# Half-row matmuls in turns on both row halves, and an RWKV chunk inverse applied ahead of the recurrence

## The chip, the cores and the metric

The kernel runs on one core of a Trainium2 chip. The metric is device time in microseconds (us) of one execution. Durations below come from one profiled execution of the kernel before, unless a sentence says that they are medians of several runs.

## What is computed

Two layers of a hybrid decoder trunk on 512 tokens of width 1024, all in float32. Each layer is a token mixer of four head groups, cross-attention into 256 memory tokens, and a SwiGLU FFN; a last RMS norm follows.

```
for each layer:
    p = rms_norm(x) @ w_in
    y = concat(rglru(p_a), retention(p_b), rwkv7(p_c), ssd(p_d))
    x = x + y @ w_out
    x = x + cross_attention(rms_norm(x), mem)
    x = x + (silu(h @ w_gate) * (h @ w_up)) @ w_down,  h = rms_norm(x)
out = rms_norm(x) * norm_final
```

The change is mostly in the RWKV-7 group, four heads of width 64. Per token and head its state S obeys

```
sa = S @ (-kk);   S = S * w + sa (kk*a)^T + v k^T;   y = S @ r
```

Retention rotates q and k: the two 32-row halves of each head are exchanged, multiplied by a sine table and added to the product with the cosine table.

## The kernel before

**Dense products.** Every large product is three fp32r matmuls (high and low parts, `mm3`, L677): a weight tile of 1024 x 128 is loaded by SyncE (SP) into a `u` buffer, ScalarE casts its high part to `v`, VectorE subtracts the low part into `w` (`weights`, L662), and 24 matmuls of 512 columns accumulate into an `a` bank of PSUM (`project`, L687). There are three buffers of each kind. The dense matmuls of the program form one chain in program order.

**Everything else on TensorE** is small plain float32 work in `b` banks (five of them): transposes, sums and the products of the mixers. A float32 matmul is two MATMUL instructions in the trace. Products with 64 rows of contraction use one half of the array's rows (form 64*128 or 64*64 in the profile), those with 64 outputs one half of its columns (128*64 or 64*64).

**Order.** Calls only record operations. `Sched.order` (L433) is a list planner with a cost for each operation; it picks the next operation of every engine by its modelled start, class and longest path to the end, gives out the buffers, and writes a fixed order for each engine. So one engine's instructions never overtake each other, and all instructions carry the source line of the helper that issues them, L569; groups are told apart by tile names and shapes. A `b` bank is only given out when two others stay free, unless the operation is the next in program order (`place`, L541).

**RWKV.** `rwkv_pair` (L1131) runs for two pairs of heads. Two low-rank products (`zw`, `za`, L1137) take lower and upper row halves; eight 64-row products per half of the tokens build the matrices inside the 64-token chunks (L1192 to L1201), first all of one head, then all of the other, each head with a bank of its own. `rwkv_solve` (L1232) inverts 32 x 32 triangles on GpSimd and carries the result (`rf`) and its transpose (`rt`) through DRAM to two tiles each. `rwkv_whole` (L1289) completes the 64 x 64 inverses by two products per cell (16 cells for each pair). `rwkv_scan` (L1310) walks over the eight chunks; for each chunk:

```
1348   E.matmul(zb[:, ...], pairs[i][0][hf][:, ccol], st[i], ...)              # state into z and y
1350   E.matmul(zb[rw[i], oc(i, o)], pairs[i][1][hf, o][:, zcol], u[:, i, hd(o)], ...)
1351   V.tensor_copy(z[rw[0]], zb[rw[0], 0:P])
1355   E.matmul(ub[rw[i], oc(i, o)], Rs[i][rw[i], n * HD:...], z[rw[i], hd(o)], ...)
1356   A.copy(u[rw[0], 0], ub[rw[0], 0:P])
1361   E.matmul(ub[:, sc], pairs[i][2][hf][:, ccol], u[:, i], ...)              # new state
1364   V.scalar_tensor_tensor(new, ub[:, sc], w, self.con("bones"), ...)
1369   E.matmul(zb[ry[i], oc(i, o)], pairs[i][1][hf, o][:, ycol], u[:, i, hd(o)], ...)
```

**Retention** (L1041) exchanges the 32-row blocks with four SP DMAs for each of four tiles (L1057), and in each of four chunks forms the scores of two heads on the lower rows and then of two on the upper rows (L1074 to L1078).

**Last norm** (`finish`, L1602). The token halves are finished one after the other. For each, sums over partitions (L1625, L1626), a root on ScalarE, a transpose that spreads it to all partitions (L1638), a ScalarE copy of it to `rb` (L1640), eight multiplies of 128 x 256 shared by VectorE (tiles 0, 2, 4, 6, 7) and GpSimd (1, 3, 5), and four SP DMAs to the output (L1648).

Of the kernel before, what the change touches and what calls it, by code (L numbers as in the profile page):

```python
# [14 lines left out]
ALU = mybir.AluOpType  # L15
# [219 lines left out]
class Op:  # L235
    __slots__ = ("n", "eng", "fn", "args", "kw", "dur", "lat", "preds", "succ", "left", "ready", "end", "rank", "cls",
                 "roots", "first", "chain", "bytes", "start", "table", "grid", "port", "fine")
# [27 lines left out]
KINDS = {"s": (T, 71), "n": (1024, 1), "t": (16, 64), "q": (P, 14), "u": (KD * P + 16, 3), "v": (KD * P + 16, 3), "w": (KD * P + 16, 3),  # L265
# [3 lines left out]
class Sched:  # L269
# [94 lines left out]
    @staticmethod  # L364
    def area(x):
        return (0, 1, 0, 1) if x.root.kind == "d" else x.box()
# [11 lines left out]
    def cost(self, op, fn, out, ins):  # L378
# [3 lines left out]
        op.table = op.grid = None  # L382
# [8 lines left out]
        elif op.eng == "PE":  # L391
# [4 lines left out]
            else:  # L396
# [7 lines left out]
                if min(k, m) <= HD:  # L404

                    op.dur /= 2
        elif op.eng == "ACT":
# [25 lines left out]
    def order(self, reserve):  # L433
# [27 lines left out]
        grid = P, P  # L461
# [4 lines left out]
        while len(out) < len(ops):  # L466
            best = None
            for e, lst in avail.items():
                c = clock[e]
                pick, pt = None, INF  # L470
                for op in lst:
# [9 lines left out]
                    key = (t, op.cls if op.cls != 2 or side < 1500.0 else 0, op.grid != grid if e == "PE" else False, -op.rank, op.n)  # L481
# [19 lines left out]
            if e == "PE" and op.grid != grid:  # L501
                t += self.change(grid, op.grid)
                grid = op.grid
            end = clock[e] = t + op.dur
# [67 lines left out]
class Trunk:  # L572
    def __init__(self, ctx, tc, a):
# [9 lines left out]
        self.d = {}  # L583

# [456 lines left out]
    def retention(self, l, proj, vals):  # L1041
# [8 lines left out]
        for which in range(2):  # L1050
            for i in range(2):
# [13 lines left out]
        for j in range(4):  # L1065
# [65 lines left out]
    def rwkv_pair(self, l, i, lora, wa, k, r, v, nd):  # L1131
# [5 lines left out]
        for z, rw in ((zw, slice(0, HD)), (za, slice(HD, P))):  # L1137
            self.mm3(z, [x[rw, cs] for x in lora], [x[rw] for x in wa], True, True)
# [53 lines left out]
        for hf in range(2):  # L1192
            for o in range(2):
                b = self.bank()
                rw = slice(HD * o, HD * o + HD)
                for c in range(4):
                    cc = slice(c * P, (c + 1) * P)
                    E.matmul(b[:, cc], bk[hf][rw, cc], ar[hf][rw, cc], start=True, stop=True)
# [33 lines left out]
    def rwkv_solve(self, l, nd):  # L1232
# [41 lines left out]
        return res  # L1274
# [471 lines left out]
```

## Time and profile before

| what | us |
|---|---|
| median of three runs | 1658.06 (1657.96 to 1658.47) |
| the profiled execution | 1656.97 |
| its span, first to last instruction | 1655.2 |
| TensorE busy | 1626.0 |
| VectorE busy | 1015.0 |
| ScalarE busy | 640.0 |
| GpSimd busy | 67.1 |

The profiled execution is 1.77 us longer than its span and 1.09 us shorter than the median. The granted TensorE clock over the span was 0.995 of full speed. Matmuls are pipelined and overlap in the trace, so what one costs is the step from its start to the next start.

### The profile page before, as it was taken

The numbers are of one execution on the slowest core, as the hardware profiler recorded it, in microseconds if no ns is written. First come the engines' busy times: TensorE is split into PE (matmuls) and PEld (weight loads), VectorE is DVE, ScalarE is ACT, GpSimd is POOL, SyncE is SP. The second block draws the span as 40 slices with busy tenths as digits, with TensorE's granted clock in tenths as the row PEclk, the third lists the DMA queues.
The fourth block names the chain that finished last, engine by engine and source line by source line (L and its number), as shares of the span: only waits on it lengthen the run. The fifth ranks groups of instructions, "written<-read, shape, count | busy, mean of one in ns | idle before, by whom it ended". The sixth has DMA issues, their size and how long they took to land.

```text
span 1655.2 us, 21468 instructions
## 1 busy us (share of the span) xinstructions
PE 1626.0 (98%) x8344; PEld 1329.1 (80%) x8344; DVE 1015.0 (61%) x1816; ACT 640.0 (39%) x988; POOL 67.1 (4%) x140
## 2 busy tenths in 40 slices
PE   7999999999999999999999999999999999999997
PEld 6787778888788888888888877888888888888886
DVE  8867699666565454533478678977565654544333
ACT  7434355444343232322354344554444322322221
POOL 0024000000000000000000600000000000000001
PEclk9999999999999999999999999999999999999999
DMA  9345203523233333233463442144233333333331
GB/s 283 114 102 123 76 26 88 180 77 87 82 99 89 101 90 102 86 106 115 133 179 99 110 99 58 52 140 141 64 90 91 100 89 102 89 97 88 92 101 56
DMA packets 315078, 169.57 MB, mean 102 GB/s; under 512 B 40160, under 2 KB 302560, under 8 KB 314848
## 3 DMA queue, kind: packets, MB, share of 16 engines
q1 hardware_dynamic: 314976, 168.19, 35.5%
q8 instruction: 66, 1.08, 0.3%
q14 instruction: 36, 0.29, 0.1%
HBM read 156.63 MB, written 9.44 MB: 100 GB/s over the span
## 4 chain that ended last, share of the span: by engine, by line
PE 92%; DVE 2%; DMA 2%; ACT 1%; SPq 1%; issue 0%; DVEq 0%; ACTq 0%
PE a L569 84%; PE b L569 9%; DVE s L569 2%; SPq L569 1%; ACT s L569 1%; DMA u<-in_mem_wk_dram 1%; DMA u<-in_w_in_dram 1%; DVE w L569 0%; DMA s<-fd 0%; DVE t L569 0%; ACT v L569 0%; DMA s<-in_memT_dram 0%; DMA s<-s 0%; ACT n L569 0%; DVEq L1742 0%
## 5 line engine op out<-in xcount | busy, mean ns | idle before, releaser
L569 PE MATMUL a<-s,v 128*128 128x512 f32 (+1 forms) x4012 | 1237.2, 388 | 8.5 <-ACT s L569 6.3
L569 PEld LDWEIGHTS a<-s,v 128*128 128x128 f32 x4012 | 741.5, 189 | 166.6 <-ACT s L569 6.9
L569 PE MATMUL a<-s,w 128*128 128x512 f32 (+1 forms) x2006 | 776.6, 387 | 0.6 <-DVE w L569 0.6
L569 ACT CAST v<-u 128x1024 fp32r<-128x1024 f32 (+3 forms) x275 | 282.6, 1028 | 663.2 <-PE a L569 380.5
L569 PEld LDWEIGHTS a<-s,w 128*128 128x128 f32 x2006 | 378.4, 189 | 80.9 <-issue 1.8
L569 DVE TENSOR_TENSOR w<-u,v 128x1024 fp32r<-128x1024 f32 (+3 forms) x275 | 329.5, 1199 | 163.6 <-ACT v L569 162.6
L569 DVE TENSOR_TENSOR s<-a,s 128x512 f32<-128x512 f32 (+1 forms) x132 | 90.6, 690 | 263.3 <-PE a L569 242.2
L569 ACT ACTIVATE s<-s 128x512 f32<-128x512 f32 (+3 forms) x233 | 144.3, 628 | 121.0 <-DVE s L569 113.7
L569 DVE TENSOR_TENSOR s<-s,s 128x512 f32<-128x512 f32 (+4 forms) x223 | 140.8, 639 | 18.2 <-ACT s L569 13.5
L569 PE MATMUL b<-s,s 128*64 128x64 f32 (+8 forms) x1268 | 134.6, 270 | 6.2 <-DVE s L569 3.5
L569 PEld LDWEIGHTS b<-s,s 128*128 128x128 f32 (+3 forms) x1268 | 111.5, 167 | 34.4 <-issue 9.1
L569 DVE SCALAR_TENSOR_TENSOR s<-s,s 128x512 f32<-128x512 f32 (+2 forms) x168 | 111.4, 669 | 10.9 <-ACT s L569 10.1
L569 DVE TENSOR_TENSOR s<-s,a 128x512 f32<-128x512 f32 (+1 forms) x49 | 33.2, 677 | 92.5 <-PE a L569 92.5
L569 PE MATMUL a<-v,s 128*128 128x260 f32 (+1 forms) x256 | 67.5, 344 | 0.0
L569 DVE SCALAR_TENSOR_TENSOR s<-s,prm,s 128x512 fp32r<-128x512 f32 (+3 forms) x78 | 53.1, 697 | 3.5 <-ACT s L569 3.1
L569 ACT COPY s<-b 64x128 f32<-64x128 f32 (+3 forms) x92 | 29.9, 335 | 63.3 <-PE b L569 47.4
L569 DVE SCALAR_TENSOR_TENSOR s<-a,prm,s 128x511 f32<-128x511 f32 (+2 forms) x64 | 47.7, 745 | 2.3 <-ACT s L569 1.4
L569 PEld LDWEIGHTS a<-v,s 128*128 128x128 f32 x256 | 44.3, 188 | 5.7
L569 PE MATMUL b<-cst,s 128*128 128x128 f32 (+2 forms) x312 | 46.3, 263 | 2.2 <-DVE s L569 1.1
L569 PEld LDWEIGHTS b<-cst,s 128*128 128x128 f32 x312 | 38.9, 157 | 9.7 <-DVE s L569 2.4
L569 PE MATMUL a<-w,s 128*128 128x512 f32 (+1 forms) x128 | 43.7, 342 | 0.0
L569 ACT CAST s<-s 128x512 fp32r<-128x512 f32 x48 | 29.1, 621 | 34.0 <-DVE s L569 27.4
(92 smaller groups left out, 667.6 us busy)
## 6 DMA issues: line engine op xcount, KB each, us to landing
u<-in_ffn_w_in_dram SPq DMA_DIRECT2D x88, 512.0 KB, 3.7
u<-in_w_in_dram SPq DMA_DIRECT2D x52, 512.0 KB, 3.8
u<-in_ffn_w_out_dram SPq DMA_DIRECT2D x32, 512.0 KB, 3.9
u<-in_mem_wv_dram SPq DMA_DIRECT2D x16, 512.0 KB, 3.6
u<-in_w_out_dram SPq DMA_DIRECT2D x16, 512.0 KB, 4.0
u<-in_mem_wq_dram SPq DMA_DIRECT2D x16, 512.0 KB, 3.9
u<-in_mem_wo_dram SPq DMA_DIRECT2D x16, 512.0 KB, 3.9
u<-in_mem_wk_dram SPq DMA_DIRECT2D x13, 512.0 KB, 4.0
```

What stands on the lines that cost most here:

```text
L569: op.fn(*[real(x) for x in op.args], **{k: real(x) for k, x in op.kw.items()})
```

## The change

- Row halves in turns: in `rwkv_pair` the three low-rank products of `zw` and `za` alternate; the 64-row products of two heads alternate, with two banks taken together (`hold`); retention's scores likewise. The planner also prefers, among small matmuls of one form, one on another part of the array than the last.
- `rwkv_solve` carries `rf` through DRAM ahead of `rt`.
- `rwkv_whole` now forms the whole inverse (its other quarter copied into a unit matrix `unit`, ScalarE) and multiplies it into the rows of `at` and `bt` that the recurrence reads, for each pair 16 + 16 + 32 products of 64 x 64 in place of 16 + 16, with ScalarE copies in between.
- `rwkv_scan`: the z products of all chunks go ahead of the recurrence (`zv`); a chunk then has a state product, an addition on VectorE, the product to the new state and its scaling; the y products follow once for each four chunks and are added on VectorE.
- Rotary exchanges are issued by ScalarE.
- Last norm: all eight multiplies on VectorE, straight from PSUM; no ScalarE copy; output DMAs in turns from SP and ScalarE; the sums that don't need the last tile come first.

```diff
-KINDS = {... "q": (P, 14), ...
+KINDS = {... "q": (P, 6), ...
+    def hold(op, x):
+        op.roots.append(x.root)
+        op.first.append(x.root)
+        x.root.uses += 1
...
-                    key = (t, ..., op.grid != grid if e == "PE" else False, -op.rank, op.n)
+                    key = (t, ..., (op.grid != grid, op.part is not None and op.part == part) if e == "PE" else (), -op.rank, op.n)
...
-                    self.Q.dma_start(s[o:o + 32], c[32 * b:32 * b + 32])
+                    A.dma_start(s[o:o + 32], c[32 * b:32 * b + 32])
...
-            for o in range(2):
-                b = self.bank()
-                rows = slice(HD * o, HD * o + HD)
-                for i in range(2):
-                    E.matmul(b[:, i * P:(i + 1) * P], k[i][rows, tk], q[i][rows, tk], start=True, stop=True)
+            bs = self.bank(), self.bank()
+            for i in range(2):
+                for o, b in enumerate(bs):
+                    rows = slice(HD * o, HD * o + HD)
+                    op = E.matmul(b[:, i * P:(i + 1) * P], k[i][rows, tk], q[i][rows, tk], start=True, stop=True)
+                    if i == o == 0:
+                        self.s.hold(op, bs[1])
...
-        for z, rw in ((zw, slice(0, HD)), (za, slice(HD, P))):
-            self.mm3(z, [x[rw, cs] for x in lora], [x[rw] for x in wa], True, True)
+        for n, (a, b) in enumerate(((0, 0), (0, 1), (1, 0))):
+            for z, rw in ((zw, slice(0, HD)), (za, slice(HD, P))):
+                E.matmul(z, lora[a][rw, cs], wa[b][rw], start=(n == 0), stop=(n == 2))
...
-        for k, f in enumerate((rt, rf)):
+        for k, f in ((1, rf), (0, rt)):
...
-            V.tensor_tensor(x[:, c2::2]..., b..., self.con("lower")..., op=ALU.mult)
+        for c3 in range(2):
+            p0 = rows(c3).start + 32
+            A.copy(x[p0:p0 + 32]..., b[p0:p0 + 32]...)
         b = self.bank()
         for c in cells:
-            E.matmul(b[rows(c[3]), col(c)], x[rows(c[3]), col(c)], R[rows(c[3]), col(c)], start=True, stop=True)
-        V.tensor_tensor(R, b, R, op=ALU.add)
+            E.matmul(b[rows(c[3]), col(c)], R[rows(c[3]), col(c)], x[rows(c[3]), col(c)], start=True, stop=True)
+        inv = TT
+        A.copy(inv, b)
+        for hf in range(2):
+            b = self.bank()
+            for q in range(2):
+                for o in range(2):
+                    for rw, e in cells:
+                        E.matmul(b[rw, ...], inv[rw, col((hf, o, q))], bt[hf][rw, x0:x0 + HD], start=True, stop=True)
+                    for rw, e in cells:
+                        E.matmul(b[rw, ...], inv[rw, col((hf, o, q))], at[hf, o][rw, self.ycol(i, q, e)], start=True, stop=True)
+            for c3 in range(2):
+                A.copy(bt[hf][rw]..., b[rw, 0:2 * P]...)
+            for c3 in range(2):
+                for o in range(2):
+                    A.copy(at[hf, o][rw]..., b[rw, 2 * P + o * P:2 * P + (o + 1) * P]...)
...
+            for q in range(2):
+                for o in range(2):
+                    for e in range(2):
+                        for i in range(2):
+                            E.matmul(b[rw[i], ...], pairs[i][1][hf, o][ry[i], self.zcol(i, q, e)], uv[hf, e][ry[i], i, q, hd(o)], start=True, stop=True)
+            A.copy(zv[:, hf], b)
...
+                if c:
+                    E.matmul(b[:, ic], pairs[i][0][hf][:, ccol], st[i], start=True, stop=True)
+                    V.tensor_tensor(u[rw[i], i], b[rw[i], ic], zc, op=ALU.add)
+                    A.copy(yt[i][ry[i], q * P:(q + 1) * P], b[ry[i], ic])
...
+                    E.matmul(b[:, sc], pairs[i][2][hf][:, ccol], u[:, i], start=True, stop=True)
...
+            if c % 4 == 3:
+                b = self.bank()
+                ...
+                                E_ = E.matmul(b[ry[i], ...], pairs[i][1][hf, o][:, self.ycol(i, x, e)], uv[hf, e][:, i, x, hd(o)], start=True, stop=True)
+                for i in range(2):
+                    V.tensor_tensor(yt[i]..., yt[i]..., b..., op=ALU.add)
...
-            rb = self.S()[:, :H]
-            A.copy(rb, b[:, :H])
...
-                    if j + k in shared:
-                        G.tensor_tensor(t[:, k], xg[j + k][:, ts], rb, op=ALU.mult)
-                    else:
-                        V.scalar_tensor_tensor(t[:, k], ..., rb, op0=ALU.mult, op1=ALU.mult)
-                self.Q.dma_start(out[...], t)
+                    V.scalar_tensor_tensor(t[:, k], ..., b[:, :H], op0=ALU.mult, op1=ALU.mult)
+                (A if j % 4 else self.Q).dma_start(out[...], t)
```

## Rows read from the trace of the kernel before

**Rows 1.** The page: busy engines, and the chain that ended last.

```profile
PE 1626.0 (98%) x8344; PEld 1329.1 (80%) x8344; DVE 1015.0 (61%) x1816; ACT 640.0 (39%) x988; POOL 67.1 (4%) x140
...
PE 92%; DVE 2%; DMA 2%; ACT 1%; SPq 1%; issue 0%; DVEq 0%; ACTq 0%
```

**Rows 2.** TensorE's waits over the span: total us, times, longest.

```profile
PE a L569 <- ACT s L569: 6.3, 2, 5.7
PE b L569 <- DVE s L569: 4.6, 6, 1.9
...
PE b L569 <- DMA s<-fd: 1.9, 2, 1.7
```

**Rows 3.** Timeline of TensorE, layer 0, 64-row groups: start, us, instruction, count.

```profile
71.64 0.40 PE L569 MATMUL a<-s,v 128*128 128x512 f32 x1
71.96 1.83 PE L569 MATMUL b<-s,s 64*128 64x128 f32 x28
73.72 0.49 PE L569 MATMUL a<-s,v 128*128 128x512 f32 x1
...
97.03 1.71 PE L569 MATMUL b<-s,s 64*128 64x128 f32 x16
98.66 0.39 PE L569 MATMUL a<-v,s 128*128 128x260 f32 x1
...
251.71 0.71 PE L569 MATMUL b<-s,s 64*128 64x128 f32 x4
252.35 0.51 PE L569 MATMUL a<-s,v 128*128 128x512 f32 x1
252.69 0.39 PE L569 MATMUL a<-s,w 128*128 128x512 f32 x1
252.92 0.63 PE L569 MATMUL a<-s,v 128*128 128x512 f32 x2
```

**Rows 4.** The same timeline, 64-column products of the RWKV group, both layers.

```profile
161.93 0.24 PE L569 MATMUL b<-s,s 64*64 64x64 f32 x1 [1.69 <-DMA s<-fd]
...
181.02 0.45 PE L569 MATMUL b<-q,s 64*64 64x64 f32 x8
181.40 0.50 PE L569 MATMUL a<-s,v 128*128 128x512 f32 x1
...
975.12 1.73 PE L569 MATMUL b<-s,s 64*64 64x64 f32 x52
976.78 0.50 PE L569 MATMUL a<-s,v 128*128 128x512 f32 x1
```

**Rows 5.** Dense matmuls (a) alone in a recurrence step, and around the low-rank products.

```profile
181.02:186.50 5.48, 4.05 (x13) 2.03 (x12) 0.00 (x0) 0.00 (x0) 1.00 0.34 96
...
49.70:53.60 3.90, 1.27 (x4) 0.52 (x4) 0.00 (x0) 0.00 (x0) 1.00 0.17 50
```

**Rows 6.** Busy us by stretch: PE, PEld, DVE, ACT, POOL, then clock and DMA.

```profile
150.00:210.00 60.00, 57.47 (x481) 43.60 (x479) 39.83 (x93) 22.07 (x51) 0.00 (x0) 0.97 0.41 90
210.00:290.00 80.00, 79.38 (x479) 64.27 (x476) 77.78 (x216) 44.35 (x76) 0.00 (x0) 1.00 0.21 61
```

**Rows 7.** Timelines: last split of a mixer output, and w_out's first matmuls.

```profile
289.56 0.69 DVE L569 SCALAR_TENSOR_TENSOR s<-s,s 128x512 fp32r<-128x512 f32 x1
...
289.43 0.63 PE L569 MATMUL a<-s,v 128*128 128x512 f32 x2
```

**Rows 8.** Timelines of the tail, and instruction groups of VectorE for its multiplies.

```profile
1643.12 0.83 PE L569 MATMUL b<-cst,s 128*128 128x1 f32 x6 [0.96 <-ACT s L569]
...
1645.76 0.37 ACT L569 COPY s<-b 128x256 f32<-128x256 f32 x1 [1.37 <-PE b L569]
...
1649.75 1.98 SPq L569 DMA_DIRECT2D out_dram<-s  x4
...
L569 DVE SCALAR_TENSOR_TENSOR s<-s,prm,s 128x256 fp32r<-128x256 f32 x16 | 7.3, 481 | 1.1 <-ACT s L569 0.8
...
DMA to landing us min/median/max: 2.2/2.7/3.0
```

More of the change, by code (lines that the diff above doesn't have):

```diff
@@ L236 @@
     __slots__ = ("n", "eng", "fn", "args", "kw", "dur", "lat", "preds", "succ", "left", "ready", "end", "rank", "cls",
-                 "roots", "first", "chain", "bytes", "start", "table", "grid", "port", "fine")
+                 "roots", "first", "chain", "bytes", "start", "table", "grid", "part", "port", "fine")
 def _free(x):
@@ L381, in cost @@
         op.bytes = 0
-        op.table = op.grid = None
+        op.table = op.grid = op.part = None
         op.port = False
@@ L460, in order @@
         side = wire = 0.0
-        grid = P, P
+        grid, part = (P, P), None
         held = {"DVE": 0.0, "POOL": 0.0}
@@ L480, in order @@
                         t = self.place(op, t, reserve)
-                    key = (t, op.cls if op.cls != 2 or side < 1500.0 else 0, op.grid != grid if e == "PE" else False, -op.rank, op.n)
+                    key = (t, op.cls if op.cls != 2 or side < 1500.0 else 0, (op.grid != grid, op.part is not None and op.part == part) if e == "PE" else (), -op.rank, op.n)
                     if pick is None or key < pick:
@@ L500, in order @@
                 r.slot = fr.pop(i)[1]
[L501 to L504, printed above, removed]
+            dur = op.dur
+            if e == "PE":
+                if op.grid != grid:
+                    t += self.change(grid, op.grid)
+                grid, part = op.grid, op.part
+            end = clock[e] = t + dur
             if op.port:
@@ L583, in __init__ @@
         self.d = {}
+        self.unit = [None, None]
     def S(self, dt=F32):
@@ L1192, in rwkv_pair @@
         for hf in range(2):
[L1193 to L1198, printed above, removed]
+            bs = self.bank(), self.bank()
+            for c in range(4):
+                cc = slice(c * P, (c + 1) * P)
+                for o in range(2):
+                    rw = slice(HD * o, HD * o + HD)
+                    op = E.matmul(bs[o][:, cc], bk[hf][rw, cc], ar[hf][rw, cc], start=True, stop=True)
+                    if c == o == 0:
+                        self.s.hold(op, bs[1])
+            for o, b in enumerate(bs):
                 t = self.S()
@@ L1273, in rwkv_solve @@
         self.solved = done
-        return res
+        return [r[::-1] for r in res]
     @staticmethod
@@ L1298, in rwkv_whole @@
             E.matmul(b[rows(c[3]), col(c)], at[c[0], c[1]][rows(c[3]), self.zcol(i, c[2], c[3] ^ i)], TT[rows(c[3]), col(c)], start=True, stop=True)
-        x = self.S()
-        for c2 in range(2):
-            V.tensor_tensor(x[:, c2::2].rearrange("p (n k w) -> p n k w", n=8, k=2), b.rearrange("p (n k c w) -> p n k c w", n=8, k=2, c=2)[:, :, :, c2],
-                            self.con("lower")[:, c2::2].rearrange("p (k w) -> p k w", k=2).unsqueeze(1).to_broadcast([P, 8, 2, 16]), op=ALU.mult)
+        if l == 0:
+            self.unit[i] = self.s.fixed([P, T], f"unit{i}")
+            V.memset(self.unit[i], 0.0)
+            for c3 in range(2):
+                rw = rows(c3)
+                A.copy(self.unit[i][rw].rearrange("p (n x) -> p n x", n=8), self.con("ident")[rw, rw].unsqueeze(1).to_broadcast([HD, 8, HD]))
@@ L1602, in finish @@
     def finish(self, xs, out):
[L1604 removed]
+        V, A, E = self.V, self.A, self.E
         ones = self.con("ones")[:, 0:1]
[L1606 to L1609 removed]
         s = None
@@ L1624, in finish @@
             for j in range(2):
-                E.matmul(b[:, j:j + 1], s[:, n * H + j * P:n * H + (j + 1) * P], ones, start=True, stop=False)
-                E.matmul(b[:, j:j + 1], sq[:, j * P:(j + 1) * P], ones, start=False, stop=True)
+                E.matmul(b[:, j:j + 1], s[:, n * H + j * P:n * H + (j + 1) * P], ones, start=(j == 0), stop=False, skip_group_check=True)
+            for j in range(2):
+                E.matmul(b[:, j:j + 1], sq[:, j * P:(j + 1) * P], ones, start=False, stop=True, skip_group_check=True)
             v = self.tiny()[:, :2]
```

98 lines of the change are left out of this document (55 added, 43 removed).

## The prediction

> **What bounds the kernel now.** I read the page first. TensorE is busy for 1626 of 1655.2 us and carries 92% of the chain that ended last [rows 1], so a change moves the time by what it takes from TensorE's queue, by what TensorE waits, and by what follows its last dense matmul. The waits come second: the longest single one, 5.7 us, is the start; beyond it TensorE waited 4.6 us for VectorE and 1.9 us for the solved blocks coming back from DRAM [rows 2]. So almost everything to win is small float32 work that stands between dense matmuls, and its cost is read from timelines by steps from start to start.
>
> A dense matmul of 512 columns steps 0.232 us (252.69 to 252.92). Into a group with 64 rows the step is 0.32 (71.64 to 71.96), and the first dense step after one is 0.34 (252.35 to 252.69) [rows 3]. So each such group costs about 0.2 us outside itself. With that added, 8 products of 64 x 64 cost 0.58 and 52 cost 1.86, so 0.029 each and 0.35 for the change of form, 0.15 of it inside the group [rows 4]. Taking 0.15 off, 28 products of 64 rows took 1.61, 0.058 each; four of one head took 0.49, 0.12 each; 16 took 1.48, 0.093 each [rows 3]. Where the trace has two heads' products in turns on the two row halves they already run side by side, a pair in 0.115; where one head follows the other they take that time singly.
>
> One whole recurrence step is the stretch from 181.02 to 186.50. Of its 13 dense matmuls one began before it, so 12 x 0.232 = 2.78 us are dense and 5.48 - 2.78 = 2.70 us are side work [rows 5].
>
> **The change part by part.**
>
> *Low-rank products in turns.* The stretch of 3.90 us around them holds four dense matmuls, of which the last begins at its end; less three steps, 0.70, they cost 3.2 us [rows 5]. After: two groups of three pairs, 2 x (3 x 0.232 + 0.35) = 2.1. Gain 1.1 a layer, 2.2 us in all (bounds 0 and 2.6).
>
> *The 64-row products of `rwkv_pair`.* 64 MATMULs a layer; all in turns they cost 32 x 0.115 = 3.7 plus 0.35 for each of two to four groups, 4.4 to 5.1. Before, 28 of them already stood in turns at 1.96 with their change of form; at the rate of the group of 16 the other 36 cost 3.3 plus 0.35 for each of two groups or more, 6.0 together. I take 1.0 a layer, 2.0 us (0 to 3.6).
>
> *Retention's scores.* Eight groups of four a layer at 0.64 + 0.2 = 0.84 [rows 3], 6.7 us if each stands alone, become four groups of eight, 4 x 0.115 + 0.35 = 0.81 each, 3.2. Some of the eight will have shared a change of form, so I take 2.5 of the 3.5: 5.0 us for both layers (0 to 7).
>
> *Recurrence.* Before, eight steps of 2.70, less a state product in the first and a new state in the last (0.46 each: four MATMULs of full form, which the rows don't price singly, taken at the 0.115 of a 64-row one with as many columns): 20.7 us a layer. After, a step has four MATMULs for the state product and four for the new state, no change of form, 0.92, seven times: 6.4; the y products come as two groups of 32 at 0.029 plus 0.35, 2.6. That saves 11.7 a layer. It is paid ahead of the recurrence: z products, 64 in two groups, 2 x (0.93 + 0.35) = 2.6; and `rwkv_whole` goes from 128 MATMULs to 256, 128 x 0.029 = 3.7 more and one more change of form, 0.35. Net 11.7 - 6.7 = 5.0 a layer, 10.0 us. If the z products don't pair, because they cross from one row half to the other column half, 64 x 0.029 = 1.9 a layer is lost; if the y products share their form with others, up to 1 is won.
>
> Here one rule speaks against the change. In the trace 52 products of 64 x 64, which write two halves of the same bank in turns, cost 0.029 each [rows 4]. The Trainium skill, page "TensorEngine Tiling (Array Packing)", section Restrictions and Gotchas, says that different row tiles cannot access the same PSUM bank simultaneously. The trace does not agree with it where the outputs lie on different partitions, and I go by the trace; what serial products would give stands among the rivals.
>
> *Waits ahead of the recurrence.* `rf` going first brings the tile that the first product needs earlier; the wait for it was 1.69 us in layer 0 [rows 4], and all such waits are at most 4.6 + 1.9 us [rows 2]. Against that, two more rounds of product and ScalarE copy stand in the chain of each layer; at the same wait for each, 4 x 1.69 = 6.8 lost. Between -6.8 and +6.5 I take 3 us won, as the wait in the rows is the one that goes.
>
> *Tail.* Before, SP's first output DMA was issued at 1649.75, after VectorE's last multiply, and the fourth landed 3.0 us after an issue that ended the row at 1651.73 [rows 8]: the four wait in one queue for the last multiply. After, the multiplies start where the ScalarE copy started, 1645.76. Eight at 7.3/16 = 0.456 us (the same form with nobody on GpSimd) end at 1649.4; only the last pair's DMA is left, landing 2.2 us later, 1651.6, where the fourth landed at about 1651.3 + 3.0 = 1654.2 before. Two of six sum matmuls no longer stand behind the last square, 0.83/6 x 2 = 0.28 [rows 8]. Gain 2.8 us. A multiply that reads PSUM has no row in this shape: at 0.3 us slower each it would take the gain back to 0.4.
>
> *At no cost.* The rotary exchanges leave SP, whose queue cost TensorE little; on ScalarE 32 issues at 1.98/4 = 0.5 us [rows 8] are 16 us beside an engine busy 22 of 60 us in that stretch [rows 6]. What covers them is the weight casts being ahead by up to three buffers. The unit tiles and the smaller pool cost nothing on TensorE.
>
> The sum: 2.2 + 2.0 + 5.0 + 10.0 + 3 + 2.8 = 25.0 us. From the profiled execution, 1656.97, that gives 1632.0; from the median, which stands 1.09 higher, 1633.1, rounded **1633**.
>
> **The rivals.**
>
> *VectorE ends the mixer.* From 210 to 290 it is busy for 77.8 of 80 us, though only 39.8 of 60 before that [rows 6]. The last split of a mixer output starts at 289.56 and takes 0.69; `w_out` begins at 289.43, and reaches the last quarter of its 24 matmuls 18 x 0.232 = 4.2 later, at 293.6 [rows 7]. So the slack is 3.4 us, and a layer's 11.1 us of gain needs 8 of the 20 us that VectorE idles before 210. A recurrence that is over sooner gives its work back there, which speaks for the forecast. If nothing moves, the layers gain 2 x 3.4 and the tail 2.8: 1648.5.
>
> *TensorE waits at each stage.* The inverse is now four stages of product, ScalarE copy, product. Should the fixed order hold TensorE at each for as long as it waited at 161.93, 1.69 us [rows 4], that is 2 x 4 x 1.69 = 13.5, and the 3 us are lost too: 1649.6. For it: this wait exists now. Against: dense work stands ready, and the planner knows the copies.
>
> *The pairs don't come.* Taking two of five banks at once, with two kept free, may make the planner break them up. Then 2.2 + 2.0 + 5.0 is lost: 1642.3.
>
> *Products into one bank run singly.* The z products read one row half and write the other's partitions, for which there is no row. Were all 320 products of 64 x 64 a layer to take two turns where the 52 took one, 0.058 each [rows 4], 2 x 9.3 us more make 1651.7.
>
> *ScalarE's queue turns it slower.* Each burst of four exchanges stands in order ahead of weight casts; if it waits for its tile, casts come late and TensorE starves. There are eight bursts; to be slower by over 0.2% they must hold TensorE for 25.0 + 3.3 us, 3.5 each, after three buffers of lead have gone. At 5 us each the result is 1673. That ScalarE is idle two thirds of the time [rows 6] speaks against it.
>
> **How the numbers follow.** The forecast has 0.64, with a range of its own from 1625 to 1640 by the bounds above; VectorE 0.10, waits 0.12, no pairs 0.07, one bank 0.02, the slower case 0.05. Some 0.2% (3.3 us) is about what a measurement can tell from no change. The range 1621 to 1646 reaches below by a dozen changes of form that the planner may merge, at 0.35 each, and above to the milder forms of the rivals. Faster 0.93; within 0.2% 0.03, where two rivals add up; slower 0.04.
>
> **What would show it.** Right: matmuls of form 64*128 in groups of eight in retention at some 0.8 us; a recurrence step with under 1 us of side work; 64*64 products at about 0.03 us; output DMAs from two queues, the last issued near 4 us after the spreading transposes. Wrong: TensorE idle ahead of the first recurrence step or before `w_out`; casts of weights behind ScalarE's DMA issues; 64*64 products at 0.05 us. The prediction falls if TensorE's waits grow by over 10 us, or if the changes of form are not fewer.

## The result, and the profile after

The changed kernel takes **1643.18 us** (median of 4, 1642.39 to 1644.17) beside 1658.01 for the kernel before on the same chip: ratio 0.9911, 95% interval 0.9899 to 0.9923. It is 14.8 us faster where 25.0 were forecast. The profiled execution took 1642.86 us, with a span of 1641.1. Lines have moved by eleven: L569 is now L580. In the views below, rows between two shown ones may be left out.

The page, busy engines, chain and the DMA queue of ScalarE:

```profile
PE 1614.6 (98%) x8472; PEld 1321.8 (81%) x8472; DVE 1005.1 (61%) x1816; ACT 648.7 (40%) x1015; POOL 63.3 (4%) x134
q10 hardware_dynamic: 2624, 3.15, 0.7%
PE 92%; DVE 3%; ACT 2%; DMA 2%; ACTq 1%; issue 1%; SPq 0%; DVEq 0%
```

Beside [rows 1], TensorE executes 128 matmuls more and is busy for 11.4 us less. The kernel is still bound by TensorE's queue. The waits of TensorE over the whole span (total us, times, longest), as in [rows 2]:

```profile
PE a L580 <- ACT s L580: 5.8, 1, 5.8
...
PE b L580 <- DVE s L580: 4.8, 7, 1.2
...
PE b L580 <- ACT s L580: 1.9, 5, 1.0
...
PE b L580 <- DMA s<-fd: 1.3, 2, 1.1
```

The DRAM wait got shorter, from 1.9 to 1.3, and the small products' waits for VectorE did not (4.6 before, 4.8 now). The timelines of TensorE (start, us, instruction, count, idle before) show where they went, and the groups that answer to [rows 3] and [rows 4]:

```profile
73.72 1.83 PE L580 MATMUL b<-s,s 64*128 64x128 f32 x28
...
158.77 0.30 PE L580 MATMUL b<-unit,s 64*64 64x64 f32 x2 [0.27 <-DMA s<-fd]
...
164.70 1.73 PE L580 MATMUL b<-s,s 64*64 64x64 f32 x52
...
177.84 0.38 PE L580 MATMUL b<-q,s 128*128 128x128 f32 x2
177.98 0.48 PE L580 MATMUL a<-s,w 128*128 128x512 f32 x1
178.30 0.39 PE L580 MATMUL a<-s,v 128*128 128x512 f32 x1
...
189.69 1.15 PE L580 MATMUL b<-s,s 128*64 128x64 f32 x32
193.80 0.49 PE L580 MATMUL b<-q,s 128*128 128x128 f32 x2 [1.17 <-DVE s L580]
...
209.40 0.71 PE L580 MATMUL b<-s,s 64*128 64x128 f32 x8
...
857.18 0.73 PE L580 MATMUL b<-s,s 64*128 64x512 f32 x3
...
858.27 1.19 PE L580 MATMUL b<-s,s 64*128 64x512 f32 x6
...
860.27 0.95 PE L580 MATMUL b<-s,s 64*128 64x512 f32 x3
```

Retention's eight products now take 0.71, as four did before (251.71 in [rows 3]). The wait of 1.69 at the first product behind the solved blocks [rows 4] has become 0.27; layer 1, which had none there, now has 1.05 (964.59). A new one of 1.17 stands inside the recurrence, ahead of a state product, and layer 1 has its twin (1.19 at 999.63). The low-rank products stand in groups of 3, 6 and 3 in layer 1, not in two of 6; they stood so before, too (863.23, 864.31 and 866.09).

The granted clock is a second thing to read. Two windows of the kernel before (the columns of [rows 6]: the clock is third from the end), and the wait ahead of the second:

```profile
160.00:166.00 6.00, 4.31 (x44) 3.19 (x38) 3.88 (x7) 0.60 (x2) 0.00 (x0) 0.72 0.38 59
980.00:986.00 6.00, 5.99 (x38) 4.40 (x39) 5.19 (x13) 2.50 (x6) 0.00 (x0) 0.72 0.02 2
...
980.01 0.45 PE L569 MATMUL b<-s,s 128*64 128x64 f32 x8 [1.93 <-DVE s L569]
```

Behind the wait of 1.69 us for the solved blocks in layer 0 [rows 4] and the one of 1.93 for VectorE in layer 1 the clock stood at half, its level of 1.2 GHz, for 3.4 us each, which is 1.7 us lost each time. After the change neither mixer of the profiled execution has such a stretch.

One profile is one execution, and the clock differs from one to the next. In the 29 executions of the kernel before that ran beside the first experiments, the granted clock over the span averaged 0.9938 (0.992 to 0.996), so some 10 us were lost below full clock; in the four of the changed kernel it averaged 0.9973, some 4.5 us. By this estimate, 5 to 6 of the 14.8 us are clock, and 9 to 10 are work, waits and the tail.

To compare kernels whose order differs, I cut every trace at the same dense matmuls (each kernel has 6498 of them). The two mixers run from the start of the 451st to that of the 1051st, and of the 3301st to the 4201st. From their length I take TensorE's idle gaps of over 60 ns and the time lost below full clock; what remains, the rest, is TensorE's own work. Both layers together, in us of the profiled executions, for all kernels of this study:

| kernel | median us | ratio to before | mixers | idle | clock | rest |
|---|---|---|---|---|---|---|
| before | 1658.0 | 1 | 470.2 | 6.1 | 3.4 | 460.6 |
| changed | 1643.2 | 0.9911 (0.9899 to 0.9923) | 458.2 | 6.4 | 0 | 451.8 |
| last norm alone | 1656.7 | 0.9983 (0.9975 to 0.9992) | 472.0 | 7.1 | 5.1 | 459.8 |
| turns alone | 1651.5 | 0.9955 (0.9941 to 0.997) | 463.8 | 6.3 | 0 | 457.5 |
| recurrence alone | 1658.4 | 1.0 (0.9991 to 1.0008) | 468.7 | 8.2 | 1.7 | 458.8 |
| exchanges alone | 1657.4 | 0.9992 (0.9982 to 1.0001) | 470.1 | 7.3 | 3.4 | 459.4 |
| turns and recurrence | 1651.6 | 0.996 (0.9948 to 0.9973) | 462.9 | 8.5 | 0 | 454.3 |
| changed, exchanges on SP | 1649.3 | 0.9943 (0.9931 to 0.9956) | 464.2 | 9.9 | 0 | 454.3 |
| changed, banks not held | 1653.4 | 0.9972 (0.996 to 0.9983) | 466.3 | 7.1 | 0 | 459.3 |
| changed, low-rank bank held | 1645.1 | 0.9926 (0.9914 to 0.9939) | 461.3 | 6.8 | 0 | 454.5 |
| changed, allowance 500 ns | 1643.2 | 0.9912 (0.9899 to 0.9926) | 461.6 | 8.4 | 1.7 | 451.5 |
| changed, allowance 350 ns | 1642.5 | 0.9903 (0.9888 to 0.9918) | 457.7 | 5.0 | 0 | 452.8 |
| changed, old order of halves | 1643.8 | 0.9912 (0.9899 to 0.9926) | 460.3 | 8.1 | 0 | 452.2 |
| changed, reads in two queues (another chip) | 1648.4 | 0.9941 (0.9925 to 0.9957) | 464.1 | 9.6 | 5.1 | 449.4 |

From before to changed the span falls by 14.1: the mixers give 12.0 (work 8.8, clock 3.4, idle -0.3), the tail 2.9, and the other parts of the kernel take 0.8 back. The last kernel of the table ran on another chip, where the kernel before takes 1660.1.

The work of the mixers by form, from the start of each matmul to the start of the next, waits and clock taken out, layer 0 / layer 1. Layer 0's stretch begins behind its low-rank and pair products, so its 64*128 row is retention alone; layer 1's has all three:

| form | before | after |
|---|---|---|
| 64*128 (retention; layer 1 also low-rank and pair products) | 4.5 / 11.5 | 2.6 / 9.6 |
| 128*64 (z, y, others) | 9.4 / 9.5 | 4.7 / 4.7 |
| 64*64 (inverse, `rwkv_whole`, z) | 8.5 / 7.9 | 12.1 / 12.1 |
| 128*128, small | 29.8 / 35.7 | 29.3 / 34.3 |
| dense | 147.6 / 196.3 | 146.7 / 195.8 |
| changes of form | 86 / 99 | 47 / 61 |
| dense row broken, times | 72 / 84 | 71 / 89 |

### The profile page after: what moved, and what is told of

Same layout as the page of the kernel before. It is cut to its first block, busy times and chain, and to the rows that moved or that the text cites. A ratio compares the mean times of both kernels' runs of the same rounds, so it can differ in the third digit from the quotient of the medians.

```text
span 1641.1 us, 21694 instructions
## 1 busy us (share of the span) xinstructions
PE 1614.6 (98%) x8472; PEld 1321.8 (81%) x8472; DVE 1005.1 (61%) x1816; ACT 648.7 (40%) x1015; POOL 63.3 (4%) x134
## 4 chain that ended last, share of the span: by engine, by line
PE 92%; DVE 3%; ACT 2%; DMA 2%; ACTq 1%; issue 1%; SPq 0%; DVEq 0%
PE a L580 83%; PE b L580 9%; DVE s L580 2%; ACT s L580 1%; DMA s<-s 1%; ACTq L580 1%; DVE w L580 0%; ACT v L580 0%; SPq L580 0%; DMA u<-in_mem_wk_dram 0%; DMA s<-in_memT_dram 0%; DMA s<-fd 0%; DVE t L580 0%; DVE q L580 0%; DVE unit L580 0%
## 5 line engine op out<-in xcount | busy, mean ns | idle before, releaser
L580 PE MATMUL a<-s,v 128*128 128x512 f32 (+1 forms) x4012 | 1237.6, 388 | 8.0 <-ACT s L580 5.8
L580 PEld LDWEIGHTS a<-s,v 128*128 128x128 f32 x4012 | 742.4, 189 | 165.3 <-ACT s L580 6.5
L580 PE MATMUL a<-s,w 128*128 128x512 f32 (+1 forms) x2006 | 775.7, 387 | 0.8 <-DVE w L580 0.8
L580 ACT CAST v<-u 128x1024 fp32r<-128x1024 f32 (+3 forms) x275 | 282.5, 1027 | 664.4 <-PE a L580 389.5
L580 PEld LDWEIGHTS a<-s,w 128*128 128x128 f32 x2006 | 378.9, 189 | 78.7 <-DVE w L580 1.2
L580 DVE TENSOR_TENSOR w<-u,v 128x1024 fp32r<-128x1024 f32 (+3 forms) x275 | 329.1, 1197 | 162.7 <-ACT v L580 162.0
L580 DVE TENSOR_TENSOR s<-a,s 128x512 f32<-128x512 f32 (+1 forms) x132 | 90.4, 689 | 263.3 <-PE a L580 244.9
L580 ACT ACTIVATE s<-s 128x512 f32<-128x512 f32 (+3 forms) x233 | 144.5, 628 | 105.0 <-DVE s L580 97.2
L580 DVE TENSOR_TENSOR s<-s,s 128x512 f32<-128x512 f32 (+3 forms) x223 | 140.3, 635 | 16.1 <-ACT s L580 12.6
L580 PEld LDWEIGHTS b<-s,s 64*64 64x64 f32 (+3 forms) x1396 | 107.4, 161 | 29.7 <-issue 7.4
L580 PE MATMUL b<-s,s 64*64 64x64 f32 (+8 forms) x1396 | 129.5, 262 | 1.7 <-DVE s L580 0.6
L580 DVE SCALAR_TENSOR_TENSOR s<-s,s 128x512 f32<-128x512 f32 (+2 forms) x168 | 109.9, 661 | 14.9 <-ACT s L580 14.3
L580 DVE TENSOR_TENSOR s<-s,a 128x512 f32<-128x512 f32 (+1 forms) x49 | 33.2, 677 | 93.2 <-PE a L580 93.2
L580 PE MATMUL a<-v,s 128*128 128x260 f32 (+1 forms) x256 | 67.1, 343 | 0.0
L580 ACT COPY s<-b 64x128 f32<-64x128 f32 (+3 forms) x122 | 39.6, 340 | 50.1 <-PE b L580 38.1
L580 ACT CAST s<-s 128x512 fp32r<-128x512 f32 x48 | 29.1, 619 | 52.3 <-DVE s L580 42.7
L580 DVE SCALAR_TENSOR_TENSOR s<-a,prm,s 128x511 f32<-128x511 f32 (+2 forms) x64 | 47.5, 742 | 3.2 <-ACT s L580 2.6
L580 PE MATMUL b<-cst,s 128*128 128x128 f32 (+2 forms) x312 | 47.2, 263 | 2.2 <-ACT s L580 1.0
L580 PEld LDWEIGHTS a<-v,s 128*128 128x128 f32 x256 | 44.3, 188 | 5.5
L580 PEld LDWEIGHTS b<-cst,s 128*128 128x128 f32 x312 | 38.9, 158 | 10.5 <-DVE s L580 2.7
L580 DVE SCALAR_TENSOR_TENSOR s<-s,prm,s 128x512 fp32r<-128x512 f32 (+2 forms) x68 | 45.8, 683 | 1.3 <-ACT s L580 1.2
L580 PE MATMUL a<-w,s 128*128 128x512 f32 (+1 forms) x128 | 43.6, 341 | 0.0
```

Of the source, the lines that this page charges most:

```text
L580: op.fn(*[real(x) for x in op.args], **{k: real(x) for k, x in op.kw.items()})
```

## The experiments

**The parts alone.** Four kernels, each the kernel before with one part of the diff.

The last norm alone (the hunks of `finish`):

> Only the new last norm on the kernel before. Account by steps: 2.8 us faster (2.3 to 3.3), all of it after the last dense matmul; the last output DMA issued near 3.7 us after the spreading transposes. Rival, the multiplies from PSUM are slower than those from SBUF: gain under 1 us. Rival, any change gives the planner another order and the total moves by that: the stretch ahead of the last dense matmul moves by over 1 us too.

It gave 1.9 us by the medians and 2.8 by the ratio, 0.9983. The tail as such is right: from the last dense matmul's start to the end of the span, 13.3 before, 10.1 here and 10.4 in the changed kernel. In its profile the clock was at half three times ahead of the tail, once more than before, and the stretch ahead of the last dense matmul took 3.0 us more. That is the sign of the second rival, but the clock alone lost 3.4 more there. The tail of the changed kernel, all engines:

```profile
1631.94 0.61 PE L580 MATMUL b<-cst,s 128*128 128x1 f32 x4 [0.96 <-ACT s L580]
...
1634.35 3.22 DVE L580 SCALAR_TENSOR_TENSOR s<-s,prm,b 128x256 f32<-128x256 f32 x8 [0.59 <-PE b L580]
1635.25 1.94 SPq L580 DMA_DIRECT2D out_dram<-s  x2
1636.04 1.95 ACTq L580 DMA_DIRECT2D out_dram<-s  x2
```

Eight multiplies out of PSUM take 0.40 each, no slower than the 0.456 from [rows 8]. The last issue ends 1638.0, 4.1 us after the spreading transposes at 1633.91.

The turns alone (planner, `hold`, retention, low-rank and pair products):

```diff
-                    E.matmul(b[:, i * P:(i + 1) * P], k[i][rows, tk], q[i][rows, tk], start=True, stop=True)
+                    op = E.matmul(b[:, i * P:(i + 1) * P], k[i][rows, tk], q[i][rows, tk], start=True, stop=True)
+                    if i == o == 0:
+                        self.s.hold(op, bs[1])
```

> Only the row halves in turns (low-rank products, 64-row products, retention) and the planner's preference. Prediction on record: 9.2 us faster. Theory after the trace of the changed kernel: retention 4.7, the 64-row products of layer 0 1.0, the low-rank products nothing since they still stand as 3, 6 and 3 matmuls: 5.7 us faster (4.5 to 7). Rival, the gain of the changed kernel is all from the recurrence: under 2 us.

7.2 us, a little above the 4.5 to 7 expected. In the profiled execution its mixers lost 3.1 us of work and the two stretches at half clock, 3.4 more, which the expectation did not have.

The recurrence alone (`rwkv_solve`, `rwkv_whole`, `rwkv_scan`, the unit tiles):

> Only the inverse applied ahead, the recurrence and the order of the solved tiles. Prediction on record: 13 us faster (10.0 and 3 of waits). Theory after the trace: 6.5 us (5 to 8), since products ahead of the recurrence stand in twelve groups a layer, not eight, and TensorE's waits are as long as before, now in front of the state products. Rival, the two parts only pay together because the preference for another part of the array is needed to pair 64 x 64 products: under 4 us, and 64 x 64 products at over 0.035 us each.

Nothing: 1658.4. The expectation fell. The rival stated there has its time but not its mark, since the 64*64 products cost 11.8 and 12.1 us a layer, as in the changed kernel (12.1). In the profiled execution TensorE's work in the mixers shrank by 1.8 us and its idle time rose by 2.1. The largest loss stands at the end of layer 0's mixer. TensorE there, ScalarE's last output of the mixer, VectorE's, and the windows:

```profile
289.91 0.50 PE L569 MATMUL a<-s,v 128*128 128x512 f32 x1 [2.75 <-ACT s L569]
...
289.22 1.23 ACT L569 ACTIVATE s<-s 128x512 fp32r<-128x512 f32 x2 [0.84 <-DVE s L569]
...
288.51 1.28 DVE L569 TENSOR_TENSOR s<-s,s 128x512 f32<-128x512 f32 x2
...
285.00:290.00 5.00, 2.25 (x13) 1.55 (x11) 4.91 (x8) 4.11 (x7) 0.00 (x0) 1.00 0.72 217
290.00:295.00 5.00, 4.77 (x13) 3.56 (x14) 1.18 (x2) 0.46 (x1) 0.00 (x0) 0.66 0.36 118
```

TensorE, in `w_out`, waits 2.75 us for the mixer's last outputs, which VectorE delivers late (4.91 of 5 us busy), and behind the wait the clock averages 0.66 of full over five us, which is 1.7 lost. This is the rival "VectorE ends the mixer". The rest of the balance is not mixer time: the two old stretches at half clock are gone, one of 1.7 us came at 42.3, and the dense matmuls between the mixers, the same in both kernels, took 1.6 more in this execution, for which the trace shows no cause. In the changed kernel the wait at `w_out` isn't there: no idle time over 60 ns precedes `w_out` in either layer.

The exchanges alone:

> Only the rotary exchanges issued by ScalarE. Prediction: nothing on TensorE, the time within 1 us of before. Rival, SP's queue was held up by them and weights came late: over 1.5 us faster. Rival, ScalarE's casts come late: over 1.5 us slower, TensorE waiting for ACT s or DVE w in the mixer.

1.2 us, by an interval that reaches 1, so neither the forecast of less than 1 us nor a small gain is excluded.

**Do the parts add up?** Their ratios multiply to 0.993, the changed kernel has 0.9911. What is missing could be the work of two parts together.

> The changed kernel without the exchanges on ScalarE and without the new last norm. Alone, the recurrence gave 0.2 us and the turns 7.2; together with the other two they gave 14.8, of which the norm's 1.9 and the exchanges' 1.2 are to be taken off. Theory 'the turns free the recurrence' (the shorter stretch of retention and of the 64-row products moves the last VectorE work of the mixer forward, so that the 2.75 us wait at w_out of layer 0 and the halved clock behind it don't come): 1646 to 1648 us, ratio 0.992 to 0.994, no TensorE wait over 0.5 us between 280 and 295. Theory 'the exchanges free it' (what clears w_out is that the rotary exchanges left SP's queue): the wait of some 2.7 us at w_out is there as in the recurrence alone, and the time is the plain sum of the two alone, 1650 to 1652 us, ratio 0.995 to 0.9965.

Neither theory as written. The wait at `w_out` is gone, so the turns do clear it, and yet the time is the plain sum, 6.6 us. The waits stand elsewhere: 0.45 and 0.76 us for the solved blocks (157.11, 160.76), 1.43 at 209.56. Then the changed kernel with only the exchanges put back on SP:

```diff
-                    A.dma_start(s[o:o + 32], c[32 * b:32 * b + 32])
+                    self.Q.dma_start(s[o:o + 32], c[32 * b:32 * b + 32])
```

> The changed kernel with the rotary exchanges back on SP's queue, all else as changed. The changed kernel stands at 0.9911 of the one before, turns and recurrence without exchanges and norm at 0.996, the norm alone at 0.9983. Theory 'the exchanges pay only beside the new recurrence' (on SP's queue they stand with the write-back and the reading of the solved blocks, so that the products ahead of the recurrence start late): the gain of turns, recurrence and norm alone remains, 0.994 to 0.995, 1648 to 1650 us, and TensorE waits over 2 us more between 150 and 215 than in the changed kernel. Rival 'the order that the planner happened to write' (each of the parts reshuffles the order, and one of them fell badly): within 2 us of the changed kernel, 0.9905 to 0.9925, 1642 to 1645.5.

1649.3, the first theory by its time: beside the new recurrence the exchanges are worth 5 to 6 us (ratios 0.9943 and 0.9911, intervals apart). SP's queue of this kernel shows one way to it, with TensorE's waits below it:

```profile
146.89 1.97 SPq L580 DMA_DIRECT2D fd<-n  x2
148.96 1.28 SPq L580 DMA_DIRECT2D s<-s  x2
150.91 2.25 SPq L580 DMA_DIRECT2D s<-s  x2
153.20 8.47 SPq L580 DMA_DIRECT2D s<-fd  x16
...
156.55 0.30 PE L580 MATMUL b<-s,s 64*64 64x64 f32 x2 [0.82 <-DMA s<-fd]
160.27 0.30 PE L580 MATMUL b<-unit,s 64*64 64x64 f32 x2 [0.83 <-DMA s<-fd]
...
209.26 0.46 PE L580 MATMUL b<-q,s 128*128 128x128 f32 x2 [1.46 <-DVE q L580]
```

In the changed kernel the queue goes straight on:

```profile
146.96 1.89 SPq L580 DMA_DIRECT2D fd<-n  x2
150.57 9.60 SPq L580 DMA_DIRECT2D s<-fd  x16
```

Four exchanges (`s<-s`) stand between the write-back of the solved blocks and their reading, which so begins 2.6 us later. TensorE is idle for 9.9 us in the mixers instead of 6.4, 1.4 of the difference at the solved blocks, and its work is 2.5 longer, with 2.6 more in small products of full form (30.6 and 35.7 us by layer, where the table has 29.3 and 34.3) and 1.0 less in dense ones. The edit also made the planner write another order: by tile names and forms TensorE's instructions differ at 962 of 8472 places, from 150.2 us on. So that the exchanges decide is shown; how much of it is the queue and how much the order is not, as no run changed the one without the other. The page "DMA: Bandwidth & Descriptors" of the Trainium skill, section "Issuing engines are not separate DMA queues", says that issuing from several engines saves only the sequencer's time, which is usually small relative to the DMA itself. In this case it is the issuing time that moved, and it was not small: 16 issues of small reads take 9.60 us on SP, ahead of the chain that starts the recurrence, and the exchanges put their start off by another 2.6.

**More in two queues?** That pointed to the reads themselves. Every second one went to ScalarE:

```diff
-                    self.Q.dma_start(t3[p0:p0 + B, :, c0:c0 + B], fd[f0:f0 + 8].rearrange("n s t -> s n t"))
+                    (A if m % 2 else self.Q).dma_start(t3[p0:p0 + B, :, c0:c0 + B], fd[f0:f0 + 8].rearrange("n s t -> s n t"))
```

> The changed kernel with every second read of the solved blocks from DRAM (8 of 16 a layer) issued by ScalarE instead of SP. Putting the exchanges back on SP's queue delayed the first of those reads from 150.6 to 153.2 in layer 0 and cost 6 us in all. Theory 'the queue of the solved blocks sets the start of the recurrence': 16 reads take 9.6 us to issue on SP (150.6 to 160.2) and 10.6 in layer 1; in two queues the last is out some 4 us sooner, the waits ahead of the unit tiles' products (0.24 and 1.02 us) go, and the mixers end 0.5 to 1.5 us sooner each: 1640 to 1642.2 us, ratio 0.9892 to 0.9904. Rival 'with the exchanges gone from SP the reads are covered': what remains of the waits stands inside the recurrence, 1642.5 to 1644.5 us, ratio 0.9905 to 0.992, and the eight issues on ScalarE, 4 us, only delay its copies.

Both theories fell: 1648.4 on another chip, by the ratios 5 us slower than the changed kernel (by the medians beside the kernel before on each chip, 3). ScalarE's queue and TensorE in layer 1, with the clock behind the wait:

```profile
956.54 4.04 ACTq L580 DMA_DIRECT2D s<-fd  x4
960.62 0.37 ACT L580 COPY s<-b 64x256 f32<-64x256 f32 x1 [6.33 <-DMA s<-fd]
...
961.04 0.32 PE L580 MATMUL b<-s,s 64*64 64x64 f32 x2 [2.30 <-ACT s L580]
...
962.00:972.00 10.00, 9.79 (x78) 6.76 (x76) 3.06 (x6) 3.86 (x8) 0.00 (x0) 0.51 0.50 111
```

A read that isn't ready yet stands in order on ScalarE ahead of a copy that TensorE needs. ScalarE idles 6.33 us, TensorE 2.30, and for ten us behind it the clock is at half, 5 us lost. TensorE's work is the least of all kernels here, 449.4, so the clock is what this variant loses by: its six executions were granted 0.991 to 0.995, those of the changed kernel 0.996 to 0.998. In layer 0 the same wait took 1.89. It is the rival "ScalarE's queue", with other DMAs. The exchanges of the change don't do this, as their data come from ScalarE's own copy just ahead of them.

**The order of the two halves.**

> The changed kernel with the two halves of the solved inverse written back in the old order, transposed one first. Theory 'the order of the halves removed the wait ahead of the recurrence' (1.66 us at 160.2 before, not there after): the wait comes back with the lower clock behind it, 1.5 to 4 us more, 1644.7 to 1647 us, ratio 0.992 to 0.9935. Rival 'what removed it is that the values' products stand ahead and cover it': within 0.7 us of the changed kernel, 1642.5 to 1643.9, ratio 0.9905 to 0.9915.

1643.8, the rival by its time: the old order is no slower than can be measured. By the mechanism it is the theory, in layer 0: the waits at the unit tiles' products, 0.27 and 1.05 us in the changed kernel, are 1.28 and 1.37 here, with TensorE's written order unchanged. But the clock stays full behind them. The profiled mixers are 2.1 us longer, 1.7 of it idle time; the medians differ by 0.6. The same wait in the two parts alone, recurrence first (its exchanges are still on SP), then exchanges:

```profile
166.37 0.29 PE L569 MATMUL b<-unit,s 64*64 64x64 f32 x2 [0.35 <-DMA s<-fd]
...
171.59 0.69 PE L569 MATMUL b<-s,s 64*64 64x64 f32 x8 [2.10 <-DMA s<-fd]
```

**What holds the pairs together.** First the changed kernel without its two calls of `hold`:

> The changed kernel without the two places where the first product of a group holds the group's second bank; the products are still written in turns on the two row halves. Theory 'turns need both banks at once' : the planner gives the second bank later, pairs break up as the low-rank ones did, retention's groups of eight at 0.84 us and the groups of 28 become smaller ones with their own changes of form, 2 to 5 us more, 1645 to 1648 us, ratio 0.992 to 0.994. Rival 'the written turns and the planner's rule for the other half are enough': 1642.5 to 1644.5, ratio 0.9905 to 0.9915, groups of the same size.

1653.4, ten us more than the changed kernel, beyond the theory's 2 to 5. The groups of 28 are unchanged, so those never needed it. Retention falls back, from four groups of eight a layer to nine of six, four and two:

```profile
208.30 0.71 PE L580 MATMUL b<-s,s 64*128 64x128 f32 x6
...
219.38 0.71 PE L580 MATMUL b<-s,s 64*128 64x128 f32 x4
...
222.89 0.48 PE L580 MATMUL b<-s,s 64*128 64x128 f32 x2
```

Work in the mixers rises by 7.5 us, 5.0 of it in matmuls of form 64*128, so retention's gain hangs on taking both banks at once. The low-rank products have no such hold, and they were given one:

```diff
-                E.matmul(z, lora[a][rw, cs], wa[b][rw], start=(n == 0), stop=(n == 2))
+                op = E.matmul(z, lora[a][rw, cs], wa[b][rw], start=(n == 0), stop=(n == 2))
+                if n == 0 and z is zw:
+                    self.s.hold(op, za)
```

> The changed kernel, with the second bank of the low-rank products held from the first one on, as retention and the 64-row products hold theirs. Theory 'the pairs were only missing a bank': all six products of a pass run in turns, three pairs instead of three pairs and six singles over a pass of two tiles (9 to 6 steps of 0.36), so 1.1 us a layer and 1641 us in all (1640 to 1642.5), ratio 0.9898 (0.989 to 0.991); the groups at 50.7, 51.6 and 53.6 become two groups of six at some 1.15 us each. Rival 'the bank is what the low-rank products lack anyway': the held bank delays another product, same time or slower, 1643 to 1646.

The pairs come, and the time doesn't: 1645.1. The groups now, and `w_out` of layer 1:

```profile
857.84 0.51 PE L580 MATMUL b<-s,s 64*128 64x512 f32 x2
858.70 0.73 PE L580 MATMUL b<-s,s 64*128 64x512 f32 x4
860.26 0.97 PE L580 MATMUL b<-s,s 64*128 64x512 f32 x6
...
1093.68 0.50 PE L580 MATMUL a<-s,v 128*128 128x512 f32 x1 [0.95 <-DVE s L580]
```

Twelve products take 2.21 us instead of 2.87. But the order of everything behind has changed, the mixers hold 2.7 us more work, and `w_out` waits for VectorE again.

**Room for the recurrence's answers.** The waits ahead of state products might come from too tight an order:

```diff
-            lat = a.lat + (200.0 if data and b.eng == "PE" and b.cls == 1 else 0.0)
+            lat = a.lat + (500.0 if data and b.eng == "PE" and b.cls == 1 else 0.0)
```

> The changed kernel, with the allowance that the planner adds to a result of another engine on its way to a recurrence product raised from 200 to 500 ns, so that more dense work is put between a result and the product that takes it. Theory 'the order is too tight' (TensorE waits 0.3 to 1.2 us ahead of state products since the planned result comes later on the chip): those waits shrink by half or more, some 2 to 4 us less, 1639 to 1641.5 us, ratio 0.988 to 0.990. Rival 'VectorE is full in the recurrence' (13.45 of 15 us busy from 180 to 195): the steps stretch with the allowance, the waits move to another place, 1643 to 1648 us, ratio 0.991 to 0.994.

> The changed kernel with the planner's allowance for a result on its way to a recurrence product at 350 ns, between the 200 of the change and the 500 tried before. At 500, layer 0 took 9.3 us less than before up to the end of its mixer (6.6 in the changed kernel), and layer 1 gave it back: 1.8 us of waits at w_out and a halved clock behind them. Theory 'the gain is there as long as the mixer's last outputs are in time': with no wait over 0.3 us at either w_out, 1639 to 1641.5 us, ratio 0.988 to 0.990. Rival 'which wait is left is the luck of the order, VectorE being full from 225 on': 1642 to 1646 us, ratio 0.9905 to 0.993, with waits of 1 us or more at one w_out or ahead of the recurrence.

1643.2 and 1642.5: neither can be told from the changed kernel. With 500 the waits stay (0.97 at 176.18, 1.16 at 184.12), and `w_out` of layer 1 waits twice, with the clock behind it:

```profile
1088.58 0.49 PE L580 MATMUL a<-s,v 128*128 128x512 f32 x1 [0.90 <-ACT s L580]
1089.99 0.80 PE L580 MATMUL a<-s,v 128*128 128x512 f32 x1 [0.92 <-DVE s L580]
...
1090.00:1093.00 3.00, 3.00 (x7) 2.43 (x8) 0.54 (x1) 0.00 (x0) 0.00 (x0) 0.50 0.79 254
```

With 350 no `w_out` waits and the mixers idle least of all, 5.0 us, but the work is 1.0 longer. So what was won here is under 1 us, inside what can be measured. Most of the changed kernel's waits are for VectorE; its windows, DVE third:

```profile
180.00:195.00 15.00, 13.52 (x108) 10.49 (x106) 13.45 (x43) 4.90 (x11) 0.00 (x0) 1.00 0.26 71
225.00:240.00 15.00, 15.00 (x84) 12.36 (x84) 15.00 (x35) 9.11 (x15) 0.00 (x0) 1.00 0.13 36
```

It is busy for 13.45 of 15 us in the recurrence and without a gap behind it. Taking VectorE's work away was not tried, so that this is the cause of the waits is argued, not shown.

## Why the prediction was right or wrong

**Right in kind, 10 us too large.** The forecast (faster through TensorE's small products and the tail) held, and so did most of its marks: groups of eight in 0.71, `w_out` without a wait, two output queues, 52 products of 64*64 at 1.73 as before. The mark of a recurrence step with under 1 us of side work was missed (below, an estimate of 1.3). The time lies inside 1621 to 1646, but outside 1625 to 1640, the range that the forecast had for itself. Part of the gain is luck as far as the forecast goes: it priced neither the clock nor the exchanges, each worth some 5 us. The time nearest to the measured one, 1642.3, belongs to "the pairs don't come", and that is chance: retention's pairs came.

- *Tail*, 2.8: measured 2.9 in the profile, and alone 1.9 by the medians, 2.8 (1.3 to 4.1) by the ratio. Right.
- *Retention*, 5.0: the matmuls of form 64*128 fell by 1.9 a layer, 3.8 together. Before, they stood in seven groups a layer and not eight; by [rows 3] the three that went spare up to 0.2 each outside, an estimate of 1.2 at most. With the turns alone TensorE's work in the mixers fell by 3.1. So it is 3 to 5: right in kind, at most 2 too large.
- *Pair products*, 2.0: about 1.0, all of it in layer 0, where groups of 12 and 16 (0.94 and 1.71) became one of 28 (1.83): 0.75 from start to start, and one change of form. Layer 1 already had its groups of 28 and 4 in turns; I had taken layer 0's rows for both.
- *Low-rank products*, 2.2: nothing. The step "two groups of three pairs" failed: the second bank isn't held in this place, and the planner left the pass split into 3, 6 and 3. With a hold the products themselves give 0.66 in layer 1.
- *Recurrence*, 10.0: the step "that saves 11.7" failed; "paid ahead", 6.7, was right (64*64 products rose by 3.6 and 4.2 a layer, on top of the 3.0 that the old steps set free). A layer's 128*64 products fell by 4.8, and the old step's eight 64*64 products (0.38 a step) by 3.0. The other 3.9 of the 11.7 were edges, dense and full-form matmuls made longer by a change of form beside them. Those two classes fell by only 1.5 and 1.9 a layer, retention's share in it: changes of form went from 86 to 47 and 99 to 61, but the dense row is broken as often as before, 72 to 71 and 84 to 89 times. The new step's matmuls come two at a time, each pair between dense ones, and I took 0.92 a step, 0.23 a pair. Seven state products of layer 0 stand alone between dense matmuls. Edges counted and waits left out, they cost 0.22 to 0.31 us (177.84: 0.14 to the next start, then a dense step of 0.32) and behind a wait 0.48 and 0.49, 0.32 on average. Four pairs at that are an estimate of 1.3 a step, which is 2.6 a layer over the forecast and about what is missing. The dense step averaged 0.277 over the recurrence of layer 0, hardly less than before (0.284). By form, this leaves some 2 us a layer in the changed kernel (4.8 + 1.5 - 3.6, less retention's 0.4, in layer 0); the work of the recurrence alone is 1.8 less for both layers, and beside the turns 3.2.
- *Waits*, 3 won: none. Idle time in the mixers is 6.4 against 6.1. The wait in [rows 4] did shrink, with the new recurrence (0.35 when that stands alone, 2.10 with the exchanges alone). The order of the halves has a part in it in layer 0 (1.28 with the old order), and so have the exchanges (0.82 and 0.83 with them on SP). But waits ahead of state products took its place.
- *Exchanges*, 0: the step "whose queue cost TensorE little" failed. I read a queue's cost in its waits before, and not in what the change was about to hang on it. They are worth 5 to 6 us beside the new recurrence, by queue and written order together, and without them idle time grows by 3.5, as the lower bound of the term *Waits* allowed for.

Unforeseen is the granted clock: of the profiled 14.1 us, 3.4 are the two stretches at half clock that went, less 1.7 for one that appeared at the start (25.1 us). Over all executions it is more, an estimated 5 to 6 us, as said with the result.

Of the rivals, "VectorE ends the mixer" is real, though not in the changed kernel: it cost the recurrence alone 2.75 us of waiting and 1.7 of clock, and two variants part of their gain. "TensorE waits at each stage" did not come: the longest wait ahead of the inverse's products is 1.05. "Products into one bank run singly" is refuted for outputs on different partitions: 320 products of 64*64 a layer cost 12.1 us, 0.038 each with every change of form, where the rival had 0.058. Here the trace does not bear out the rule of "TensorEngine Tiling (Array Packing)", section Restrictions and Gotchas, of the Trainium skill, that different row tiles cannot access one PSUM bank simultaneously. "The pairs don't come" held for the low-rank products alone. No variant beats the changed kernel by more than can be measured.

## What to carry to other kernels

Price a group of small matmuls by the breaks it makes in the dense row, and count those in the order that will be written, since a change of form saved was worth little here where the row stayed broken. Before calling a DMA's move between queues free, read what stands behind it in the old queue and whether the new queue would ever wait for its data. When parts of a change are planned into one order, test them together as well as alone: here two parts worth 0 and 1 us alone decide over 5 to 6 us in company. Compare the granted clock of all executions before explaining a difference by one profile.

## What the hardware showed that I had not expected

A wait of TensorE can come to 1.6 to 3.2 times what the trace calls idle. After the 2.75 us at 289.91, the 2.30 at 961.04 and the two of 0.9 at 1088.58 and 1089.99 the granted clock stood at 0.5, the level of 1.2 GHz, for 3.4, 10.2 and 3.4 us, which is 1.7, 5.1 and 1.7 us more. Not each wait does it, and its length alone doesn't tell: the 1.69 at 161.93 before was followed by half clock, an equal one at 977.50 with the exchanges alone was not, nor were the 1.17 at 193.80 and the 1.28 and 1.37 with the old order of halves. That the wait is the cause is read from what follows what; no run changed the wait alone.
